# Five more projections of the first layer take the paired form on the tensor engine

## The chip, the core and the metric

The kernel runs on one core of a Trainium2 chip. The engines named here are TensorE (PE in the profile; its weight loads are PEld), VectorE (DVE), ScalarE (ACT), GpSimd (POOL) and SyncE (SP, which here only issues DMAs). Each works through a list of instructions of its own and waits on the others through semaphores. The metric is the device time of one execution in microseconds.

## The reference

A trunk of two layers works on x of 256 x 1024 in float32. In each layer one normalised x goes through one combined input projection, and its 3584 columns feed three branches: dilated attention (8 heads), a gated linear recurrence (width 256) and stick-breaking attention (4 heads). Each branch is multiplied by a SiLU gate, and all of them go through the output projection back onto x.

```
hn = rms_norm(x, norm_gain)
proj = jnp.einsum('bsd,de->bse', hn, w_in)
a_q, a_k, a_v, a_g, b_x, b_g, c_q, c_k, c_v, c_g = jnp.split(proj, _in_split_points(), axis=-1)
y_a = dilated_attention(rope(a_q), rope(a_k), a_v) * jax.nn.silu(a_g)
y_b = rg_lru_branch(b_x, conv_w, conv_b, ...) * jax.nn.silu(b_g)
y_c = stick_breaking_attention(c_q, c_k, c_v) * jax.nn.silu(c_g)
x = x + jnp.einsum('bse,ed->bsd', concat([y_a, y_b, y_c]), w_out)
```

## The kernel before

**Products.** To keep float32 accuracy, every operand is split into a rounded part and its rest (x into `xh` and `xl`, a weight into `whi` and `wlo`), and three products are summed: rounded by rounded, rounded by rest, rest by rounded. `xh` and `xl` of the same 128 rows lie side by side in the tile `xx`, each 256 positions wide.

**Chunks.** The columns of the input projection come in chunks of 256, in a fixed order: stick-breaking q and k (CQ, CK), first dilated q and k (heads 0 to 3; AQ0, AK0), the recurrent input (BX), second dilated q and k (AQ1, AK1), the stick-breaking gate (CG), the recurrent gate (BG), two chunks of the dilated gate (AG, AG+1), then four chunks of the output projection. A chunk's weights arrive in two DMAs of 512 KB into the tiles `st` (5 of them); ScalarE rounds each quarter into `whi` (L115), VectorE subtracts to get `wlo` (L117). `whi` and `wlo` have 4 buffers each; `st` is free for the next load once L117 has read it, so loads wait on VectorE. Each chunk's weights are asked for two chunks ahead (`AHEAD`).

**Two forms of a chunk** (`proj_b`). A chunk has two halves of 128 columns. The narrow form makes 24 products of 256 columns for each half (L225) and keeps both halves in one PSUM bank of the pool `pp`. The paired form makes, for each half, 8 products 512 columns wide of `whi` with `xx`, which gives the first and the rest of x at once (L344), and 8 of 256 columns of `wlo` with `xh` (L341). The half has a bank of its own; its two sides are summed afterwards: ScalarE copies one side into the tile `low` (L347), VectorE adds it to the other (L349). Layer 1 uses the paired form for all its chunks, layer 0 so far only for the two dilated gate chunks (`PAIRED`). `pp` has three banks. A bank can be taken again only when the sum L349 (paired) or the operations that read it (narrow) are done.

**Normalisation in layer 0.** x goes into the products unnormalised; the reciprocal norms, as a row `rb`, are multiplied in afterwards (`scaled` at L413, `rotated` at L514 and L518). Layer 1 has no such product.

**Order of the work.** TensorE's instructions stand in the order in which the code writes them; VectorE's and ScalarE's lists are put together by a scheduler when the kernel is built, and are then fixed. Between the two halves of some chunks other work is put in (`mid`): in AQ1 `second()`, the scores of the first dilated heads (L542 on TensorE, then L549 and the softmax on VectorE and ScalarE), and in BG `third()`, the recurrent gates (L601), the values of two branches (L453, one of them in a bank of `pp`) and the scores of the second dilated heads (L542). The dilated probabilities are turned by L489.

Of the kernel before, what the change touches and what calls it, by code (L numbers as in the profile page):

```python
# [15 lines left out]
P = 128  # L16
S = 256
# [25 lines left out]

CH_AV, CH_CV, CH_CQ, CH_CK, CH_BX, CH_CG, CH_BG, CH_AG, CH_O = 0, 2, 3, 4, 7, 10, 11, 12, 14
CH_AQ, CH_AK = (5, 8), (6, 9)
PAIRED = ((CH_AG, CH_AG + 1), (CH_CQ, CH_CK, CH_AQ[0], CH_AK[0], CH_BX, CH_AQ[1], CH_AK[1], CH_CG, CH_BG, CH_AG, CH_AG + 1))


@with_exitstack
def trunk_kernel(ctx: ExitStack, tc: tile.TileContext, x, first_x, first, wpack, prm_d, gatew, gains, consts, rope, out):  # L50
    nc = tc.nc
    act, dve, pe, gps = nc.scalar, nc.vector, nc.tensor, nc.gpsimd
# [13 lines left out]
    def scr(w):  # L66
        return wk.tile([P, 512], F32, name="scr", tag="scr", bufs=SCR)[:, 0:w]
# [20 lines left out]
    def v2(a, n=2):  # L88
        return a.rearrange("p (b t) -> p b t", b=n)
# [58 lines left out]
    pair = None  # L148
    for k in range(NK):
# [5 lines left out]
        if k % 2 == 0:  # L155
            pair = [wsp.tile([P, 2048], F32R, name=n, tag=n) for n in ("whi", "wlo")]
        o = k % 2
# [150 lines left out]
    rb = cst.tile([P, S], F32, name="rb")  # L308
    gn = cst.tile([P, D], F32, name="gn", tag="gn")

    for l in range(L):
# [14 lines left out]
        def proj_b(c, mid=None, to=None, sc=1.0):  # L326
            pair = c in PAIRED[l]
            hi, lo = [a.rearrange("p (k c) -> p k c", c=256) for a in weights(l, c, AHEAD - 1 if mid else AHEAD)]
# [29 lines left out]
            return flat  # L358

        def proj_to(dst, c, mid=None, sc=1.0):  # L360
            if l > 0 and c in PAIRED[l]:
                proj_b(c, mid, [dst[:, b, :] for b in range(2)], sc)
            else:
                scaled(dst, proj_b(c, mid), sc)

# [44 lines left out]
        def scaled(dst, ps, sc=1.0):  # L410
            if l == 0:
                a, b = rows(ps)
                dve.scalar_tensor_tensor(dst, a, sc, b, ALU.mult, ALU.mult)  # L413
            else:
                act.activation(dst, v2(ps), AF.Copy, scale=sc)
# [9 lines left out]
        if l > 0:  # L425
            tables()

        def silu(dst, ps):
            sg = v2(scr(512))
            src = v2(ps)  # L430
            if l == 0:
                src = v2(scr(512))
                scaled(src, ps)
            tab(sg, src, AF.Sigmoid)
            dve.tensor_mul(dst, src, sg)

# [66 lines left out]
        def rotated(c, tiles, h0, tag, mid=None):  # L503
            dst = tiles[h0] = sb.tile([P, 2, S], F32, name=tag, tag=tag)
            tab_ = rp0 if l == 0 else rp
            if l > 0:
                src = scr(S)
                proj_b(c, mid, [src, dst[:, 1, :]])
            else:
                ps = proj_b(c, mid)  # L510
                src = ps[:, 0:S]
            sh = scr(S)
            dve.stream_shuffle(sh, src, SHUF)
            dve.tensor_mul(dst[:, 0, :], src, tab_[:, 0, :])  # L514
            dve.tensor_mul(sh, sh, tab_[:, 1, :])
            dve.tensor_add(dst[:, 0, :], dst[:, 0, :], sh)
            if l == 0:
                dve.tensor_mul(dst[:, 1, :], ps[:, S:2 * S], rb)  # L518

        qT, kT, exact = {}, {}, {}  # L520
        prob = {}
# [59 lines left out]
        bg = sb.tile([P, 2, S], F32, name="bg", tag="bg")  # L581
        cg = sb.tile([P, 2, S], F32, name="cg", tag="cg")
# [74 lines left out]
        rotated(CH_AK[1], kT, 4, "k1")  # L657
        split_qk(4, ("q0", "ag"))
        table(SIGM)
        cg_ps = proj_b(CH_CG)  # L660
        pts = dil_transposes(0)
        silu(cg, cg_ps)


# [5 lines left out]
            y_c["y"] = values(va, pts, 0, bank(pp, "pp"))  # L670
            y_c["s"] = dil_scores(4)

        silu(bg, proj_b(CH_BG, third))
        y_half(1)
        table(LN_EXP)
        lru_scan()
# [2 lines left out]
        ps = None  # L679
        if CH_AG in PAIRED[l]:  # L680
            agf = sb.tile([P, 2, S], F32, name="agf", tag="cg")
            proj_b(CH_AG, None, [agf[:, b, :] for b in range(2)])
            ps = agf.rearrange("p b t -> p (b t)")
        dil_softmax(y_c["s"])
        ps = proj_b(CH_AG) if ps is None else ps
# [168 lines left out]
```

## Time and profile before

| | |
|---|---|
| median of 3 runs (lowest to highest) | 246.11 us (246.09 to 246.35) |
| the profiled execution's own time | 246.06 us |
| its span in the profile | 244.2 us |
| busy share of the span: PE, PEld, DVE, ACT, POOL | 97%, 85%, 82%, 71%, 4% |
| layer 0 from its first chunk to the end of AG+1, by the chain of waits | 23.63 to 98.24 us |
| granted TensorE clock | 0.999 |

Times in the views are microseconds from the span's start. In a row of a timeline stand start, duration, engine, line, operation, output and inputs, the count, and in brackets how long the engine was idle before and what ended that. Several rows of equal instructions are merged; the start of the next row shows how long they took together, since an instruction's last part overlaps the next one's first. In the chain of waits stand start, duration, and what ran.

### The profile page before, as it was taken

What the parts mean: (1) busy time and instruction counts of PE and PEld (TensorE: products, weight loads), DVE (VectorE), ACT (ScalarE), POOL (GpSimd) and SP (SyncE); (2) the same over time, 40 slices, a digit from 0 to 9 for tenths busy, and PEclk for the clock granted to TensorE, in tenths of its full rate; (3) what the DMA queues carried; (4) which work ended last, traced back from release to release, by engine and by line L of the source; (5) the groups of instructions that cost most, each with busy time, mean ns of one, the idle gap of its engine ahead of it and who ended that gap; (6) DMA issues with size and microseconds to landing.
All of it is one profiled execution on the core that took longest, in us unless ns stands there. A gap on an engine that the chain in (4) does not pass through costs nothing.

```text
span 244.2 us, 4576 instructions
## 1 busy us (share of the span) xinstructions
PE 236.2 (97%) x1651; PEld 206.6 (85%) x1651; DVE 200.0 (82%) x480; ACT 174.4 (71%) x384; POOL 10.5 (4%) x43
## 2 busy tenths in 40 slices
PE   8799999999999999999999999999999999999991
PEld 4588999999999798878888888888888878887881
DVE  3694699999999889999495585999999986997362
ACT  3677987919597689994673674876669867998143
POOL 0017200002000000000000000000010000000000
PEclk9999999999999999999999999999999999999999
DMA  6989988565846843068448288615470771000022
GB/s 193 377 254 390 384 268 291 190 205 177 240 152 207 272 153 105 1 195 320 175 134 273 88 289 268 199 44 177 171 214 7 226 282 63 31 0 0 3 75 97
DMA packets 14037, 43.89 MB, mean 180 GB/s; under 512 B 1728, under 2 KB 3008, under 8 KB 14016
## 3 DMA queue, kind: packets, MB, share of 16 engines
q1 hardware_dynamic: 13248, 42.43, 51.9%
q0 software_dynamic: 192, 0.52, 0.8%
q10 hardware_dynamic: 576, 0.66, 0.7%
q8 instruction: 13, 0.21, 0.4%
q14 instruction: 8, 0.07, 0.1%
HBM read 42.03 MB, written 1.05 MB: 176 GB/s over the span
## 4 chain that ended last, share of the span: by engine, by line
PE 94%; DMA 3%; DVE 1%; SPq 0%; ACT 0%; issue 0%; DVEq 0%
PE pp L225 34%; PE pp L344 20%; PE pp L341 10%; PE s L225 9%; PE s L181 4%; PE s L489 3%; DMA st<-first 3%; PE y L453 2%; PE pp L383 2%; PE s L542 2%; PE pp L181 2%; PE s L469 1%; PE y L225 1%; PE pp L453 1%; PE s L601 1%; PE s L273 1%
## 5 line engine op out<-in xcount | busy, mean ns | idle before, releaser
L117 DVE TENSOR_TENSOR wlo<-st,whi 128x512 fp32r<-128x512 f32 x128 | 81.8, 684 | 7.5 <-ACT whi L115 6.9
L115 ACT ACTIVATE whi<-st 128x512 fp32r<-128x512 f32 x130 | 72.5, 627 | 9.0 <-DMA st<-w_pack 3.4
L344 PE MATMUL pp<-xx,whi 128*128 128x512 f32 x208 | 50.8, 393 | 0.0
L344 PEld LDWEIGHTS pp<-xx,whi 128*128 128x128 f32 x208 | 37.8, 188 | 7.6 <-DVE q L349 0.3
L225 PE MATMUL pp<-xx,whi 128*128 128x256 f32 x288 | 38.2, 285 | 0.0
L225 PEld LDWEIGHTS pp<-xx,whi 128*128 128x128 f32 x288 | 35.8, 191 | 0.8 <-issue 0.3
L341 PEld LDWEIGHTS pp<-xx,wlo 128*128 128x128 f32 x208 | 26.9, 191 | 1.6 <-ACT scr L84 0.3
L341 PE MATMUL pp<-xx,wlo 128*128 128x256 f32 x208 | 28.0, 284 | 0.0
L225 PE MATMUL pp<-xx,wlo 128*128 128x256 f32 x144 | 20.2, 283 | 0.0
L84 ACT ACTIVATE pr<-scr,mn 128x128 f32<-128x128 f32 (+1 forms) x32 | 14.1, 443 | 6.6 <-DVE mn L549 6.6
L225 PEld LDWEIGHTS pp<-xx,wlo 128*128 128x128 f32 x144 | 18.6, 192 | 0.0
L78 ACT ACT_TABLE_LOAD x13 | 16.7, 1283 | 1.9 <-PEq L847 1.7
L347 ACT ACTIVATE low<-pp 128x256 f32<-128x256 f32 x26 | 9.4, 373 | 8.8 <-PE pp L344 8.0
L225 PE MATMUL pp<-whi,yh 128*128 128x512 f32 (+1 forms) x48 | 14.1, 382 | 0.0
L225 PE MATMUL pp<-wlo,yh 128*128 128x512 f32 (+1 forms) x48 | 13.7, 372 | 0.0
L225 PE MATMUL pp<-whi,yl 128*128 128x512 f32 (+1 forms) x48 | 13.6, 371 | 0.0
L181 PE MATMUL s<-whi,xx 128*128 128x512 f32 (+1 forms) x36 | 9.6, 384 | 1.8 <-ACT xx L161 1.7
L225 PEld LDWEIGHTS pp<-whi,yl 128*128 128x128 f32 x48 | 8.6, 188 | 1.6
L225 PEld LDWEIGHTS pp<-wlo,yh 128*128 128x128 f32 x48 | 8.6, 188 | 1.6
L225 PEld LDWEIGHTS pp<-whi,yh 128*128 128x128 f32 x48 | 8.3, 188 | 1.6 <-issue 0.3
L549 DVE CUSTOM_DVE_ANT_0 scr<-s,con 128x128 f32<-128x128 f32 (+1 forms) x32 | 9.2, 350 | 0.0
L181 PEld LDWEIGHTS s<-whi,xx 128*128 128x128 f32 x36 | 6.0, 197 | 3.3 <-ACT xx L161 2.5
(189 smaller groups left out, 372.3 us busy)
## 6 DMA issues: line engine op xcount, KB each, us to landing
st<-w_pack SPq DMA_DIRECT2D x66, 512.0 KB, 5.3
st<-first SPq DMA_DIRECT2D x7, 512.0 KB, 7.0
xres<-x_in SPq DMA_DIRECT2D x4, 256.0 KB, 7.5
gw_t<-gate_w SPq DMA_DIRECT2D x2, 256.0 KB, 6.8
gn<-gains SPq DMA_DIRECT2D x2, 256.0 KB, 5.9
xs<-xc POOLq DMA_DIRECT2D x4, 128.0 KB, 3.8
gf<-gains SPq DMA_DIRECT2D x2, 256.0 KB, 5.4
out<-st ACTq DMA_DIRECT2D x2, 192.0 KB, 2.0
```

The source lines that it names most:

```text
L78: load = act.preload_act_table_set(name)
L84: i = dep(act.activation(*a, **k), loaded["load"])
L115: split[l, c] = act.activation(h, part, AF.Copy)
L117: dve.tensor_sub(r, part, h.bitcast(F32))
L181: pe.matmul(ps[t][:, c0:c1], a[:, k, t * P:(t + 1) * P], b, start=k == 0 and all(m[0] is not ps for m in seq[:i]), stop=k == NK - 1 and al ...
L225: pe.matmul(ps, a(k), b(k), start=first and i == 0, stop=last and i == len(seq) - 1, skip_group_check=skip)
L341: pe.matmul(ps[:, 0:S], lo[:, k, cs], xh[:, k, :], start=i == 0, stop=i == len(seq) - 1, skip_group_check=True)
L344: pe.matmul(ps, hi[:, k, cs], xx[:, k].rearrange("p h t -> p (h t)"), start=i == 0, stop=i == len(seq) - 1, skip_group_check=True)
L347: act.activation(low, ps[:, S:2 * S], AF.Copy, scale=sc)
L453: pe.matmul(y[hr, p * 128 + o:p * 128 + 256], vt[:, s0, hs], wts[i][s0], start=s0 == 0, stop=s0 == 1)
L489: pe.transpose(tp[:, i * P:(i + 1) * P], tiles[h0 + h][:, j * P:(j + 1) * P], ident)
L549: dve.tensor_tensor_reduce(xs[:, cs], sps[h][:, cs], nmask[:, cs], -0.125, 3e38, ALU.add, ALU.min, mn[:, t:t + 1])
```

## The change

In layer 0, BX, AQ1, AK1, CG and BG go from the narrow to the paired form. The sums of their halves are written where the value is to live (the convolution's input, the rotated tiles, the gates' own tiles); the product with `rb` is then made from there and no longer from PSUM. For BX that is a product in place (`proj_to`), for the gates `scaled` reads the gate's tile, for q and k the first half is summed into scratch before the rotation and the second half into its home.

```diff
-PAIRED = ((CH_AG, CH_AG + 1), (CH_CQ, CH_CK, CH_AQ[0], CH_AK[0], CH_BX, CH_AQ[1], CH_AK[1], CH_CG, CH_BG, CH_AG, CH_AG + 1))
+PAIRED = ((CH_BX, CH_AQ[1], CH_AK[1], CH_CG, CH_BG, CH_AG, CH_AG + 1), (CH_CQ, CH_CK, CH_AQ[0], CH_AK[0], CH_BX, CH_AQ[1], CH_AK[1], CH_CG, CH_BG, CH_AG, CH_AG + 1))
...
         def proj_to(dst, c, mid=None, sc=1.0):
-            if l > 0 and c in PAIRED[l]:
+            if c in PAIRED[l]:
                 proj_b(c, mid, [dst[:, b, :] for b in range(2)], sc)
+                if l == 0:
+                    dve.tensor_mul(dst, dst, rb.rearrange("p (o t) -> p o t", o=1).broadcast_to([P, 2, S]))
...
+        def home(tile_):
+            return [tile_[:, b, :] for b in range(2)] if l == 0 else None
+
         def silu(dst, ps):
             sg = v2(scr(512))
-            src = v2(ps)
+            src = dst if ps is None else v2(ps)
             if l == 0:
-                src = v2(scr(512))
-                scaled(src, ps)
+                ps, src = src, v2(scr(512))
+                scaled(src, ps.rearrange("p b t -> p (b t)"))
...
-            if l > 0:
-                src = scr(S)
-                proj_b(c, mid, [src, dst[:, 1, :]])
+            pair = c in PAIRED[l]
+            if pair:
+                src, high = scr(S), dst[:, 1, :]
+                proj_b(c, mid, [src, high])
             else:
                 ps = proj_b(c, mid)
-                src = ps[:, 0:S]
+                src, high = ps[:, 0:S], ps[:, S:2 * S]
...
             if l == 0:
-                dve.tensor_mul(dst[:, 1, :], ps[:, S:2 * S], rb)
+                dve.tensor_mul(dst[:, 1, :], high, rb)
...
-        cg_ps = proj_b(CH_CG)
+        cg_ps = proj_b(CH_CG, None, home(cg))
...
-        silu(bg, proj_b(CH_BG, third))
+        silu(bg, proj_b(CH_BG, third, home(bg)))
```

Ten sums (L349) and ten copies (L347) are added to the lists of VectorE and ScalarE, and the scheduler puts these lists together anew. Three places on VectorE follow, each before and then in the changed kernel. Lines behind the first edits have other numbers in the changed kernel: L513 to L518 are L519 to L524, L549 is L555, L413 is L415, L435 is L440, L562 is L568, L590 is L596, L617 is L623. An `ISA` row is the reduction of scores (L549).

First place: from the split of the first dilated k, over BX and its convolution, to the first reduction of scores. Before:

```order
L528 TENSOR_TENSOR qk_717<-k_644,qk_717 128x512
L117 TENSOR_TENSOR wlo<-st,whi 128x512 x2
L413 SCALAR_TENSOR_TENSOR bxp<-pp,rb 128x2x256
L588 TENSOR_SCALAR xc<-bxp,prm_t 128x256 x2
L590 SCALAR_TENSOR_TENSOR xc<-bxp,prm_t,xc 128x256 x2
L117 TENSOR_TENSOR wlo<-st,whi 128x512
L590 SCALAR_TENSOR_TENSOR xc<-bxp,prm_t,xc 128x256 x4
L117 TENSOR_TENSOR wlo<-st,whi 128x512 x7
L549 ISA scr,mn<-s,con 128x128
```

The same place in the changed kernel:

```order
L534 TENSOR_TENSOR qk_717<-k_644,qk_717 128x512
L349 TENSOR_TENSOR bxp<-pp,low 128x256
L117 TENSOR_TENSOR wlo<-st,whi 128x512 x2
L349 TENSOR_TENSOR bxp<-pp,low 128x256
L364 TENSOR_TENSOR bxp<-bxp,rb 128x2x256
L594 TENSOR_SCALAR xc<-bxp,prm_t 128x256 x2
L117 TENSOR_TENSOR wlo<-st,whi 128x512
L596 SCALAR_TENSOR_TENSOR xc<-bxp,prm_t,xc 128x256 x6
L349 TENSOR_TENSOR scr<-pp,low 128x256
L117 TENSOR_TENSOR wlo<-st,whi 128x512 x4
L520 TENSOR_TENSOR q_805<-scr,rp_288 128x256
L555 ISA scr,mn<-s,con 128x128
```

Three sums and a product of the rotation now stand ahead of the first reduction, and four weight splits in place of seven.

Second place: from the end of the first softmax to the rotation of the second dilated k (`q_814` and `q_805` are the second dilated q, `k_948` the second dilated k). Before:

```order
L562 TENSOR_SCALAR pr<-pr,den 128x256
L514 TENSOR_TENSOR q_814<-pp,rp_288 128x256
L515 TENSOR_TENSOR scr<-scr,rp_288 128x256
L518 TENSOR_TENSOR q_814<-pp,rb 128x256
L516 TENSOR_TENSOR q_814<-q_814,scr 128x256
L117 TENSOR_TENSOR wlo<-st,whi 128x512
L528 TENSOR_TENSOR qk_1035<-q_814,qk_1035 128x256
L117 TENSOR_TENSOR wlo<-st,whi 128x512
L513 STREAM_SHUFFLE scr<-pp 128x256
```

The same place in the changed kernel:

```order
L568 TENSOR_SCALAR pr<-pr,den 128x256
L349 TENSOR_TENSOR q_805<-pp,low 128x256
L522 TENSOR_TENSOR q_805<-q_805,scr 128x256
L524 TENSOR_TENSOR q_805<-q_805,rb 128x256
L117 TENSOR_TENSOR wlo<-st,whi 128x512 x4
L349 TENSOR_TENSOR scr<-pp,low 128x256
L349 TENSOR_TENSOR k_948<-pp,low 128x256
L519 STREAM_SHUFFLE scr<-scr 128x256
```

The sum of AQ1's second half stands behind the whole softmax, and four weight splits stand between it and the sums of AK1's two halves. By the banks that the built kernels use, the first half of CG takes the bank of AQ1's second half, the second half of CG that of AK1's first half, and BG's first half that of AK1's second.

Third place: from the last reduction of the second scores to the sum of AG's first half (`agf`). Before:

```order
L549 ISA mn 128x1
L413 SCALAR_TENSOR_TENSOR scr<-pp,rb 128x512
L117 TENSOR_TENSOR wlo<-st,whi 128x512 x2
L435 TENSOR_TENSOR bg<-scr 128x512
L117 TENSOR_TENSOR wlo<-st,whi 128x512 x2
L617 TENSOR_TENSOR scr<-av 128x512
L349 TENSOR_TENSOR agf<-pp,low 128x256
```

The same place in the changed kernel:

```order
L555 ISA mn 128x1
L349 TENSOR_TENSOR bg<-pp,low 128x256
L415 SCALAR_TENSOR_TENSOR scr<-bg,rb 128x512
L117 TENSOR_TENSOR wlo<-st,whi 128x512 x2
L440 TENSOR_TENSOR bg<-scr 128x512
L117 TENSOR_TENSOR wlo<-st,whi 128x512
L623 TENSOR_TENSOR scr<-av 128x512
L349 TENSOR_TENSOR agf<-pp,low 128x256
```

The sum of BG's second half stands ahead of the gate's product with `rb`, and one weight split has gone behind. The first half of AG+1 takes the bank of AG's first half in the changed kernel as before it.

## The prediction

> **What bounds the kernel now.** I read the page first: its span, the busy shares, VectorE's slices and the chain that ended last.
>
> ```profile
> span 244.2 us, 4576 instructions
> PE 236.2 (97%) x1651; PEld 206.6 (85%) x1651; DVE 200.0 (82%) x480; ACT 174.4 (71%) x384; POOL 10.5 (4%) x43
> DVE  3694699999999889999495585999999986997362
> PE 94%; DMA 3%; DVE 1%; SPq 0%; ACT 0%; issue 0%; DVEq 0%
> ```
>
> TensorE sets the time: 94% of the chain is its own work. But from the sixth slice to the thirteenth (6.1 us each, 30 to 79 us) VectorE stands at 9 as well, so it is the second bound of just the stretch that is changed. The windows of that stretch say how full it is; the columns behind the times are length, then PE, PEld, DVE and ACT busy.
>
> ```profile
> 51.68:58.75 7.07, 7.07 (x65) 6.94 (x62) 7.03 (x17) 4.39 (x9) 0.41 (x4) 1.00 0.56 186
> 58.75:64.40 5.65, 5.65 (x76) 5.51 (x77) 5.65 (x16) 2.95 (x8) 1.25 (x2) 1.00 0.81 243
> 64.40:70.20 5.80, 5.80 (x50) 5.80 (x50) 5.80 (x31) 5.77 (x19) 0.00 (x0) 1.00 0.76 254
> ```
>
> VectorE has 0.04 us free in 18.5; ScalarE has 5.4. Next the chain in order of time, for layer 0 and, below the second dots, two pieces of layer 1, which has the paired form already.
>
> ```profile
> 32.71 5.75 PE pp L225 x48
> ...
> 58.75 1.37 PE s L542 x38
> 60.12 14.59 PE pp L225 x120
> 74.71 1.31 PE s L489 x12
> 76.02 2.86 PE pp L225 x24
> 78.88 1.02 PE s L601 x16
> ...
> 84.02 3.06 PE pp L225 x24
> 87.08 1.84 PE pp L344 x8
> 88.92 1.91 PE pp L341 x16
> 90.83 3.65 PE pp L344 x16
> ...
> 98.24 2.73 PE s L225 x12
> ...
> 183.01 3.83 PE pp L344 x16
> ...
> 206.57 3.70 PE pp L344 x16
> ```
>
> TensorE runs through layer 0 without a gap. In layer 1, 16 wide products take 3.83 us once and 3.70 once, against 3.65 in AG: 0.18 and 0.05 us lost, both where a half must wait for a bank.
>
> **What the change saves.** A narrow half is 24 products: 5.75 / 2 = 2.88 us. A paired half is 8 wide, 3.65 / 2 = 1.83, and 8 narrow, 1.91 / 2 = 0.95: 2.78 us. Columns streamed are as many as before (12288 per chunk); only the cost per product falls away, for 8 products fewer: 0.10 us per half, 1.0 us for ten. The Trainium skill (TensorE: Matmul & The Clock Gate, section "Wait — 56ns, not 53.3ns?") has the start-to-start time of a warm product at its columns over 2.4 GHz plus 2.5 ns; by that rule the saving would be an estimated 10 x 8 x 2.5 ns = 0.2 us, and rivals 1 and 2 below would come out 0.8 us later. The rows give 120 ns for 256 columns and 228 for 512, so 11 to 12 ns per product here; I go by them.
>
> **What it adds.** Per form, from the grouped view:
>
> ```profile
> L117 DVE TENSOR_TENSOR wlo<-st,whi 128x512 fp32r<-128x512 f32 x128 | 81.8, 684 | 7.5 <-ACT whi L115 6.9
> L347 ACT ACTIVATE low<-pp 128x256 f32<-128x256 f32 x26 | 9.4, 373 | 8.8 <-PE pp L344 8.0 <-PE pp L341 0.8
> L349 DVE TENSOR_TENSOR scr<-pp,low 128x256 f32<-128x256 f32 x12 | 4.9, 418 | 0.7 <-ACT low L347 0.7
> ```
>
> Ten copies are 3.7 us on ScalarE, which lie in its free time. Ten sums are 10 x 0.42 on a VectorE that has no free time. The products with `rb` and the rotation cost the same from either memory, so they are moved, not added, save that BX's product now must wait for its sum. Banks matter more: a paired half gives its bank back only after copy and sum, and the sums stand in VectorE's list behind other work. So I walk VectorE's list of the changed kernel with the durations of before. These rows are VectorE's, layer 0 and, below the first dots, layer 1, with one row of PEld last.
>
> ```profile
> 53.23 0.68 DVE L528 TENSOR_TENSOR qk<-k,qk 128x512 fp32r<-128x512 f32 x1
> 55.77 0.74 DVE L588 TENSOR_SCALAR xc<-bxp,prm_t 128x256 f32<-128x256 f32 x2
> 59.40 4.29 DVE L117 TENSOR_TENSOR wlo<-st,whi 128x512 fp32r<-128x512 f32 x7
> 63.62 0.28 DVE L549 CUSTOM_DVE_ANT_0 scr<-s,con 128x128 f32<-128x128 f32 x1
> ...
> 178.61 0.42 DVE L514 TENSOR_TENSOR q<-scr,rp 128x256 f32<-128x256 f32 x1
> 178.94 0.28 DVE L549 CUSTOM_DVE_ANT_0 scr<-s,con 128x128 f32<-128x128 f32 x1
> ...
> 184.25 0.42 DVE L349 TENSOR_TENSOR q<-pp,low 128x256 f32<-128x256 f32 x1
> ...
> 184.72 1.69 PEld L344 LDWEIGHTS pp<-xx,whi 128*128 128x128 f32 x8 [0.30 <-DVE q L349]
> ```
>
> Start to start, a split costs 0.60 us ((63.62 - 59.40) / 7) and a 256-wide operation 0.33. Before, the scores of the first dilated heads were done at 60.12, but their reduction began at 63.62, behind seven splits: the order of the list decides, not readiness.
>
> *First bank (CG's first half waits for the sum of AQ1's second half).* The split of k starts at 53.23 as before, the next at 53.84. Sum 0.33, two splits 1.2, sum 0.5 with its wait for `low` and for its result, product 0.73: L588 starts at 56.6, 0.85 later than before. Its convolution and one split take 3.63 (55.77 to 59.40): 60.25. Sum 0.33, four splits 2.4, rotation 0.33: the reduction starts at 63.35. From there the list is layer 1's, where the sum starts 5.31 us later (178.94 to 184.25) and ends at 0.42: bank free at 69.1. TensorE: three halves have gained 0.3 by then, so the scores run 58.45 to 59.82; AQ1's second half takes 2.98 (layer 0 has the same 0.2 after L542: 3.06 against 2.88), AK1 5.56: it wants the bank at 68.36. In layer 1 the products start 0.35 after the sum's end (184.67 to 183.01 + 1.83 + 0.18 = 185.02), so here at 69.45. **Stall 1.1 us.**
>
> *Second bank (CG's second half waits for the sum of AK1's first half).* After 68.7 come the sum, two operations and four splits: 3 x 0.33 + 2.4, then this sum 0.42: free at 72.5, products at 72.9. TensorE wants it at 69.45 + 2.78 = 72.25. **Stall 0.65 us.**
>
> *Third bank (AG+1's first half waits for the sum of AG's first half).* Rows of before, VectorE first, then ScalarE:
>
> ```profile
> 84.44 0.28 DVE L549 CUSTOM_DVE_ANT_0 scr<-s,con 128x128 f32<-128x128 f32 x1
> ...
> 87.12 0.69 DVE L413 SCALAR_TENSOR_TENSOR scr<-pp,rb 128x512 f32<-128x512 f32 x1 [0.38 <-PE pp L225]
> ...
> 91.74 0.42 DVE L349 TENSOR_TENSOR agf<-pp,low 128x256 f32<-128x256 f32 x1
> ...
> 117.64 0.69 DVE L744 TENSOR_TENSOR xres<-pp,xres 128x512 f32<-128x512 f32 x1 [1.67 <-PE pp L225]
> ...
> 88.26 0.61 ACT L84 ACTIVATE scr<-scr 128x512 f32<-128x512 f32 x1
> 88.89 1.28 ACT L78 ACT_TABLE_LOAD   x1
> ```
>
> Before, that sum ended at 92.16, and 0.35 later is 92.51; TensorE came at 87.08 + 5.57 = 92.65. The margin is 0.15 us. Now: from 72.45 VectorE has ten 256-wide operations (3.3) and eighteen 512-wide ones, twelve of them splits (10.8), and some 0.3 of waits until the second reductions: 86.9, where before it was 84.44. The reductions take 2.3 (87.12 - 0.38 - 84.44); the sum of BG's second half 0.45: the gate's product starts at 89.65. From there to AG's sum it was 4.62 (87.12 to 91.74); the sigmoid had waited 0.45 for ScalarE's splits (87.81 to 88.26) and now doesn't: 4.17. Sum at 93.8 to 94.25, products at 94.6. TensorE: CG ends at 72.9 + 2.78 = 75.7, L489 1.31, BG's first half 2.78, `third()` 5.14 (78.88 to 84.02), the second half 2.98, AG 5.56: 93.45. **Stall 1.15 us.**
>
> Behind it AG+1 takes 5.56 and ends at 100.15, against 98.24: later by 1.9 us. The sum of terms is the same: -1.0 + 1.1 + 0.65 + 1.15 = +1.9. What follows is off by as much on both engines, and VectorE waits for TensorE again by 117.64 (1.67 us), so the lag doesn't grow into layer 1, whose code is untouched. From the profiled execution, 246.06 us (0.05 below the median), that is **248.0 us**.
>
> **Bounds.** Saving: 0.2 below the rows' 1.0 at the worst, if the changes between wide and narrow cost more than in AG. Stalls: at least layer 1's, 0.18, 0 and 0.05; at most 0.6 more each than walked, since some 110 instructions stand in the walk. Where a stall ends on VectorE's row, TensorE's saving ahead of it doesn't count: the end of AG+1 hangs on the last stall alone, and an error of 1% in VectorE's 40 us is 0.4 us. The forecast's own range is 247.2 to 248.8.
>
> A load is the other unknown: those for AG+1 now stand behind splits that come later, and its second half can be issued at about 71.1 (the second of BG's splits), where ScalarE needs it by 74.9 ahead of the rounding of k. A load that had the queue for itself before:
>
> ```profile
> L108 SPq DMA_DIRECT2D st<-w_pack x1: 328/328/328, 72.5 to 72.5; - x1
> DMA to landing us min/median/max: 3.8/3.8/3.8
> ```
>
> At 3.8 us it lands at 74.9, just in time.
>
> **The rivals.**
> (1) *Sums hidden as in layer 1*: banks are late by 0.18 and 0.05 only, -1.0 + 0.23 = -0.8: 245.3. For it: layer 1 does the same chunks at that loss. Against: VectorE there has no products with `rb`, and the sums don't stand behind four splits.
> (2) *VectorE keeps pace, but the gate's chain is longer*: BG's copy and sum come ahead of the gate's product, 0.37 + 0.42. Products after AG's sum came 5.43 after BG's end (92.51 - 87.08), now 6.22, or 5.77 without the sigmoid's wait; TensorE comes 5.57 after it, so AG+1 stalls 0.2 to 0.65. With 0.2 at CG that is -1.0 + 0.4 to 0.85, or 245.5 to 245.9. For it: that margin. Against: the walk, by which the reductions are 2.5 us late.
> (3) *Weights late*: the load for AG+1 takes 4.7 us or more instead of 3.8; ScalarE's list stands still until it lands, the rounding of k, the second scores and AG's sum come 0.9 later at least, on top of the forecast: 248.9 upwards. For it: two loads are now issued 1.2 us apart. Against: at 72 us the queue is nearly empty.
>
> **How the numbers follow.** Forecast 0.76, rival 1 0.04, rival 2 0.10, rival 3 0.10. About 0.2% (0.5 us) is what a measurement of this kernel can tell from no change. Faster holds rival 1 and a part of rival 2: 0.08; the same holds most of rival 2 and the forecast's low edge: 0.07; slower the rest, 0.85. The range runs from 246.5, above rivals 1 and 2, to 249.2, into rival 3.
>
> **What would show it.** Right: in the chain, halves of L344 and L341 at 2.78 us; PEld waiting for L349 of q ahead of CG (1.1 us), of scr ahead of CG's second half (0.65) and of agf ahead of AG+1 (1.15); VectorE without a gap from 45 to 87 us; the second reductions near 87. Wrong: PEld waits there under 0.3 us, or the reductions start by 85 (rivals 1 and 2); ScalarE waiting for `st<-w_pack` near 75 us (rival 3); or TensorE stalled for another cause, a missing `wlo` say.

## The result, and the profile after

The changed kernel takes 247.47 us in the median (nine runs, 246.78 to 248.64), the kernel before 246.11: a ratio of 1.0067, 95% interval 1.0042 to 1.0092. It is slower by 0.4 to 0.9%; 248.0 was forecast. The profiled execution took 246.81 us. Its page, the rows that answer to those of before:

```profile
span 244.9 us, 4428 instructions
PE 236.6 (97%) x1571; PEld 202.9 (83%) x1571; DVE 203.1 (83%) x490; ACT 177.3 (72%) x394; POOL 10.5 (4%) x43
DVE  3884798999999999999695485899999986997362
PE 83%; DVE 10%; ACT 2%; DMA 2%; issue 0%; SPq 0%; DVEq 0%
```

TensorE's share of the chain fell from 94% to 83%, and VectorE's rose from 1% to 10%: the end now hangs on VectorE for a while. The chain in order of time says where (start, duration, what ran):

```profile
31.43 0.23 PE y L401 x2
...
47.76 1.84 PE pp L344 x8
49.60 0.95 PE pp L341 x8
...
64.60 1.57 ACT pr L84 x7
...
68.59 2.41 DVE wlo L117 x4
...
93.08 2.11 PE pp L344 x8
...
98.94 2.73 PE s L225 x12
...
108.47 1.45 PE y L458 x16
```

A paired half is 1.84 + 0.95 = 2.79 us, as worked out. But from 64.60 to 93.08 the chain has no TensorE in it. TensorE itself waits three times in that time, at the three places that were named. Its weight loads, with the wait ahead of them in brackets:

```profile
67.97 1.68 PEld L344 LDWEIGHTS pp<-xx,whi 128*128 128x128 f32 x8 [1.04 <-DVE q L349]
...
71.39 1.02 PEld L341 LDWEIGHTS pp<-xx,wlo 128*128 128x128 f32 x8 [0.56 <-DVE scr L349]
...
93.08 1.68 PEld L344 LDWEIGHTS pp<-xx,whi 128*128 128x128 f32 x8 [1.24 <-DVE agf L349]
```

**How much the stretch lost.** The two profiled executions do not start alike, mostly because the first loads landed 0.84 us sooner in this one (5.41 us for 6.25 in the chain). So each execution is measured from the first product of the rows of norms, the row `31.43 ... PE y L401 x2`, to the values of the first branch behind AG+1, the row `108.47 ... PE y L458 x16`: 77.04 us. In the kernel before, the same rows stand at 32.48 and 107.77, with other line numbers: 75.29. The stretch is 1.75 us longer. What follows is as long as before to a tenth (244.9 - 108.47 = 136.43, and 244.2 - 107.77 = 136.43), and the earlier start hides 1.05. The same stretch by engine, columns as in the prediction's windows, first of before, then of after:

```profile
32.48:107.77 75.29, 75.29 (x645) 69.89 (x645) 72.14 (x184) 59.74 (x129) 1.66 (x6) 1.00 0.57 185
```
```profile
31.43:108.47 77.04, 75.26 (x564) 65.53 (x565) 74.38 (x193) 61.24 (x137) 1.67 (x6) 1.00 0.55 178
```

VectorE has 2.24 us more to do in it and takes 1.75 us longer; its free time falls from 3.15 us to 2.66. Whether this added work sets the loss or the three waits do is what the experiments ask.

### The profile page after: what moved, and what is told of

Its sections match the earlier page's. It is cut to its first block, busy times and chain, and to the rows that moved or that the text cites. A ratio compares the mean times of both kernels' runs of the same rounds, so it can differ in the third digit from the quotient of the medians.

```text
span 244.9 us, 4428 instructions
## 1 busy us (share of the span) xinstructions
PE 236.6 (97%) x1571; PEld 202.9 (83%) x1571; DVE 203.1 (83%) x490; ACT 177.3 (72%) x394; POOL 10.5 (4%) x43
## 3 DMA queue, kind: packets, MB, share of 16 engines
HBM read 42.03 MB, written 1.05 MB: 176 GB/s over the span
## 4 chain that ended last, share of the span: by engine, by line
PE 83%; DVE 10%; ACT 2%; DMA 2%; issue 0%; SPq 0%; DVEq 0%
PE pp L225 22%; PE pp L344 22%; PE pp L341 12%; PE s L225 9%; PE s L181 4%; DVE wlo L117 4%; PE s L494 3%; PE pp L385 2%; DMA st<-first 2%; PE pp L181 2%; PE y L458 2%; PE s L548 2%; PE s L474 1%; PE y L225 1%; DVE scr L555 1%; PE s L273 1%
## 5 line engine op out<-in xcount | busy, mean ns | idle before, releaser
L117 DVE TENSOR_TENSOR wlo<-st,whi 128x512 fp32r<-128x512 f32 x128 | 82.0, 683 | 8.1 <-ACT whi L115 7.5
L115 ACT ACTIVATE whi<-st 128x512 fp32r<-128x512 f32 x130 | 73.2, 628 | 8.7 <-DMA st<-w_pack 5.0
L344 PE MATMUL pp<-xx,whi 128*128 128x512 f32 x288 | 71.0, 394 | 1.4 <-DVE agf L349 0.8
L344 PEld LDWEIGHTS pp<-xx,whi 128*128 128x128 f32 x288 | 52.2, 188 | 12.4 <-DVE agf L349 1.4
L341 PEld LDWEIGHTS pp<-xx,wlo 128*128 128x128 f32 x288 | 37.3, 191 | 2.9 <-DVE scr L349 0.6
L347 ACT ACTIVATE low<-pp 128x256 f32<-128x256 f32 x36 | 13.2, 373 | 11.5 <-PE pp L344 10.7
L225 PE MATMUL pp<-xx,whi 128*128 128x256 f32 x128 | 16.8, 284 | 0.0
L225 PEld LDWEIGHTS pp<-xx,whi 128*128 128x128 f32 x128 | 15.9, 192 | 0.3 <-issue 0.3
L181 PE MATMUL s<-whi,xx 128*128 128x512 f32 (+1 forms) x36 | 10.4, 411 | 0.3 <-ACT xx L161 0.2
L555 DVE CUSTOM_DVE_ANT_0 scr<-s,con 128x128 f32<-128x128 f32 (+1 forms) x32 | 9.2, 351 | 0.0
L485 DVE TENSOR_TENSOR_SCAN sw<-scr,con 128x127 f32<-128x127 f32 (+1 forms) x16 | 8.0, 539 | 0.7 <-ACT scr L84 0.7
L568 DVE TENSOR_SCALAR pr<-pr,den 128x128 f32<-128x128 f32 (+1 forms) x32 | 8.4, 314 | 0.2
```

The source lines that it names most:

```text
L115: split[l, c] = act.activation(h, part, AF.Copy)
L117: dve.tensor_sub(r, part, h.bitcast(F32))
L181: pe.matmul(ps[t][:, c0:c1], a[:, k, t * P:(t + 1) * P], b, start=k == 0 and all(m[0] is not ps for m in seq[:i]), stop=k == NK - 1 and al ...
L225: pe.matmul(ps, a(k), b(k), start=first and i == 0, stop=last and i == len(seq) - 1, skip_group_check=skip)
L341: pe.matmul(ps[:, 0:S], lo[:, k, cs], xh[:, k, :], start=i == 0, stop=i == len(seq) - 1, skip_group_check=True)
L344: pe.matmul(ps, hi[:, k, cs], xx[:, k].rearrange("p h t -> p (h t)"), start=i == 0, stop=i == len(seq) - 1, skip_group_check=True)
```

## The experiments

Two readings were open. In one, each of the three waits is a loss of its own, and an order that takes one away gets its time back. In the other, VectorE's list sets the end, and a wait only shows where TensorE meets it. A third question was whether the kernel could keep the saving at all. In the table stand the ratio to the kernel before in runs on the same chip, then what the stretch of the last section lost against 75.29 us, and how much of it VectorE was free, both by the profiled execution. From the stretch's end to layer 1's first product are 33.50 us in the kernel before, in the change and in all other runs of the table that have a trace, but for three: e10, e11 and e12 lose 0.32, 0.10 and 0.38 us more there.

| run | ratio [95%] | stretch | VectorE free |
|---|---|---|---|
| the change | 1.0067 [1.0042, 1.0092] | +1.75 | 2.66 |
| e1_early_q_k_sums | 1.0057 [1.0035, 1.0078] | +1.52 | 3.05 |
| e2_early_ag_sum | 1.0081 [1.0056, 1.0106] | +1.86 | 2.26 |
| e3_all_three | 1.0073 [1.0052, 1.0094] | +1.85 | 2.53 |
| e4_no_sums | 1.0011 [0.9997, 1.0024] | +0.25 | 4.49 |
| e5_ten_more_sums | 1.0088 [1.0076, 1.0100] | +1.79 | 2.39 |
| e6_six_rests_on_gpsimd | 1.0144 [1.0125, 1.0163] | +4.73 | 5.37 |
| e7_bx_aq1_ak1_paired | 1.0038 [1.0023, 1.0054] | +0.92 | 3.00 |
| e8_cg_bg_paired | 1.0086 [1.0069, 1.0102] | +1.60 | 4.71 |
| e9_no_sums_o0_later | 1.0001 [0.9986, 1.0017] | – | – |
| e10_o0_later | 1.0126 [1.0105, 1.0146] | +2.44 | 5.89 |
| e11_q_k_sums_and_o0 | 1.0071 [1.0049, 1.0093] | +1.31 | 3.82 |
| e12_rewritten_lists | 1.0036 [1.0017, 1.0054] | +0.61 | 2.42 |

e9 has no trace of an ordinary execution, so its last two fields are empty. In the diffs, `dep(a, b)` puts `a` behind `b` in the order that the scheduler makes, and nothing else; `lows`, `sums`, `rests` and `rounds` hold a chunk's copies (L347), sums (L349), splits (L117) and roundings (L115), `soft` the named instructions of softmax and gates. O0 and O1 are the first two chunks of the output projection.

### Taking the waits away by order: e1, e2, e3

e1 puts AQ1's second copy ahead of the softmax's exponentials, its second sum ahead of the reciprocals, and BG's four splits behind AK1's first sum:

```diff
-        rotated(CH_AQ[1], qT, 4, "q1", second)
+        rotated(CH_AQ[1], qT, 4, "q1", second); l == 0 and [dep(soft[0, k][0], d[0, CH_AQ[1], 1]) for k, d in (("exp", lows), ("rec", sums))]
...
-        split_qk(4, ("q0", "ag"))
+        split_qk(4, ("q0", "ag")); l == 0 and [dep(i, sums[0, CH_AK[1], 0]) for i in rests[0, CH_BG]]
```

> Order alone: ScalarE's copy of AQ1's second half is put ahead of the softmax's exponentials, its sum ahead of the reciprocals, and the four splits of BG's weights behind the sum of AK1's first half. Theory (VectorE has no free time, so the end of AG+1 hangs on its row alone): the two waits ahead of CG fall from 1.04 and 0.56 us to under 0.3 each, but AG's sum stands where it stood on VectorE, within 0.3 us, so the wait ahead of AG+1 grows from 1.24 to some 2.5 us and the time stays at 247.2 to 247.5. Rival (each wait is a loss of its own): the third wait stays at 1.2 and the time falls by 1.6, to 245.9.

Both waits ahead of CG's halves are gone, 1.60 us of them, and the stretch is 0.23 us shorter than in the change. These are TensorE's waits now:

```profile
81.41 0.29 PEld L548 LDWEIGHTS s<-k,q 32*128 32x128 f32 x2 [0.50 <-ACT rt L84]
82.14 0.41 PEld L548 LDWEIGHTS s<-k,q 32*128 32x128 f32 x9 [0.44 <-ACT it L84]
...
92.67 1.68 PEld L344 LDWEIGHTS pp<-xx,whi 128*128 128x128 f32 x8 [0.99 <-DVE agf L349]
```

TensorE came to the second scores (those of the second dilated heads) sooner and waited there for the recurrent gates (`rt`, `it`), which ScalarE makes behind its other work. The wait ahead of AG+1, expected to grow to 2.5 us, fell to 0.99; the time stayed where it was expected. The page of this kernel gives VectorE 21% of the chain, in the change 10%. e2 takes the third wait away: ScalarE copies AG's first half ahead of a change of its function table.

```diff
-            proj_b(CH_AG, None, [agf[:, b, :] for b in range(2)])
+            proj_b(CH_AG, None, [agf[:, b, :] for b in range(2)]); l == 0 and dep(loaded["load"], lows[0, CH_AG, 0])
```

> Order alone: ScalarE's copy of AG's first half is put ahead of the load of the exponential's table, so that its sum comes before the product of av. Theory: the wait ahead of AG+1 falls from 1.24 us to under 0.3; the next that is late is the rest of the recurrent gate's part of y (now done 0.35 us before TensorE uses it), so the gain is 0.4 to 0.9: 246.6 to 247.1. Rival (each wait a loss of its own): 1.15 gained, 246.3. Rival (VectorE's fill alone counts, whatever the order): 247.4.

AG+1 no longer waits, and the stretch is no shorter; the expected gain of 0.4 to 0.9 us did not come. The next products wait instead, for the recurrent branch's rounded output and for the gate's product that frees their bank:

```profile
99.61 0.30 PEld L225 LDWEIGHTS s<-whi,yh 128*128 128x128 f32 x2 [0.96 <-ACT yh L446]
100.67 0.30 PEld L225 LDWEIGHTS s<-whi,yl 128*128 128x128 f32 x2 [0.31 <-DVE yl L447]
...
102.75 0.30 PEld L225 LDWEIGHTS pp<-whi,yh 128*128 128x128 f32 x2 [0.26 <-DVE scr L444]
```

0.96 + 0.31 + 0.26 = 1.53, for 1.24 taken away. The chain ahead of that rounded output runs on ScalarE from 88.89 to 96.09, over a rounding, a change of table, exponentials and the recurrent branch's `th`, so here the order on ScalarE counts and not VectorE's fill alone. e3 has both edits:

```diff
+        rotated(CH_AQ[1], qT, 4, "q1", second); l == 0 and [dep(soft[0, k][0], d[0, CH_AQ[1], 1]) for k, d in (("exp", lows), ("rec", sums))]
...
+        split_qk(4, ("q0", "ag")); l == 0 and [dep(i, sums[0, CH_AK[1], 0]) for i in rests[0, CH_BG]]
...
+            proj_b(CH_AG, None, [agf[:, b, :] for b in range(2)]); l == 0 and dep(loaded["load"], lows[0, CH_AG, 0])
```

> Both edits of order together. Theory (VectorE too full): the waits ahead of CG under 0.3 us, the one ahead of AG+1 0.5 to 1.5, since TensorE now comes 1.6 us earlier than VectorE's list can serve it, or the wait moves on to the parts of y in the output's products; 246.3 to 246.9. Rival (each wait a loss of its own): all 2.8 us gained, 244.7, below the kernel before.

All three bank waits are gone, and the time is that of the change. Its weight loads wait 0.37 and 0.44 us at the second scores, then 0.79, 0.30 and 0.27 at the places of e2. The first reading falls: the waits are not three losses that can be had back.

### The sums without the pairing, the pairing without the sums: e5, e4

e5 is the kernel before with ten 256-wide additions on VectorE, at the places of the sums and with nothing paired:

```diff
+        def more(tile_):
+            for b in range(2 if l == 0 else 0):
+                dve.tensor_add(wk.tile([P, S], F32, name="low", tag="low", bufs=2), tile_[:, b, 0:S], tile_[:, b, 0:S])
...
+            more(bxp)
...
```

> The kernel before, all chunks narrow as they were, with ten additions of 128x256 more on VectorE (two behind each of BX, AQ1, AK1, CG and BG, from and to on-chip memory, their result unused). No bank is handed back another way, and TensorE saves nothing. Theory (VectorE's fill from 38 to 92 us is the whole cause, and TensorE's saving doesn't count because VectorE sets the end): VectorE reaches AG's sum 1.5 to 2.2 us later and the ratio is that of the changed kernel, 1.005 to 1.009. Rival (what costs is that banks come back only after copy and sum): 1.000 to 1.002.

It loses as much as the change, 1.0088 against 1.0067, with intervals that overlap. TensorE has no wait at CG and one at AG+1:

```profile
93.48 1.69 PEld L344 LDWEIGHTS pp<-xx,whi 128*128 128x128 f32 x8 [1.43 <-DVE agf L349]
```

So ten short operations on VectorE cost this kernel some 2 us (248.03 against 245.97) with the banks of the five chunks handed back as before; the wait turns up at the bank of AG, which was paired already. e4 does the reverse: the five chunks stay paired, but ScalarE copies the first side home, and the second side, rest of x by rounded weight, is left out with its sums.

```diff
-                    act.activation(low, ps[:, S:2 * S], AF.Copy, scale=sc)
-                    if sc == 1.0:
+                    act.activation(*((to[b], ps[:, 0:S]) if l == 0 and c < CH_AG else (low, ps[:, S:2 * S])), AF.Copy, scale=sc)
+                    if sc == 1.0 and (l > 0 or c >= CH_AG):
...
```

> In BX, AQ1, AK1, CG and BG the sum is left out: ScalarE copies the first 256 columns of the bank straight to their home, and the product of the rest of x with the weights' high part is left out of the result (TensorE still makes it). Theory (the ten sums on VectorE are the cause): VectorE has 3.3 us less to do, the three waits fall under 0.3 us each, TensorE keeps its saving of 1.0 us: 245.1 (244.8 to 245.6). Rival (TensorE saves nothing, or the paired products cost more than their rows say): no wait, but 246.1 or more. Rival (the copies on ScalarE hold the banks): the wait ahead of CG stays at 0.5 us or more.

Without the sums the loss is gone, and there is no gain either (245.1 us had been expected, 245.82 came where the kernel before took 245.5). TensorE was ahead: its products for the recurrent gates (the first with `gw_t`) start at 77.27, 45.56 us into the stretch, where before it was 46.33 (78.81 - 32.48). It then waits at the second scores, and by 0.17 us at AG+1; besides a wait of 0.35 us at the stretch's end, which the kernel before has too, only these weight loads show a wait for another engine:

```profile
82.13 0.41 PEld L548 LDWEIGHTS s<-k,q 32*128 32x128 f32 x9 [0.44 <-ACT it L84]
...
91.86 1.69 PEld L344 LDWEIGHTS pp<-xx,whi 128*128 128x128 f32 x8 [0.17 <-DVE agf L349]
```

By the products' starts, the second scores take 2.44 us to the next product (81.04 to 83.48), where before it was 1.36 (82.59 to 83.95): 1.08 us lost in that one place. VectorE, then ScalarE, ahead of it:

```profile
73.83 3.69 DVE L117 TENSOR_TENSOR wlo<-st,whi 128x512 fp32r<-128x512 f32 x6
77.44 0.69 DVE L415 SCALAR_TENSOR_TENSOR scr<-cg,rb 128x512 f32<-128x512 f32 x1
...
78.16 0.63 ACT L84 ACTIVATE scr<-scr 128x512 f32<-128x512 f32 x1 [1.64 <-DVE scr L415]
78.70 1.66 ACT L115 ACTIVATE whi<-st 128x512 fp32r<-128x512 f32 x3
...
80.53 0.83 ACT L84 ACTIVATE rt<-s,prm_t 128x256 f32<-128x256 f32 x2
```

CG's product with `rb` stands behind six splits in VectorE's list (behind three in the change). CG's sigmoid on ScalarE waits 1.64 us for it, and behind the sigmoid stand three roundings of O0 and a copy, and only then the gates. VectorE is free for 4.49 us of the stretch, so what is late here is late by its place in a list. It also shows a limit of e4 and e5: the scheduler laid the lists of both anew, and they differ in more than the sums.

### Less work on VectorE: e6, e7, e8

e6 gives six of twelve splits of BG, AG and AG+1 to GpSimd, that is 6 x 0.60 = 3.6 us off VectorE.

```diff
-                dve.tensor_sub(r, part, h.bitcast(F32))
+                (gps if l == 0 and c in (CH_BG, CH_AG, CH_AG + 1) and j else dve).tensor_sub(r, part, h.bitcast(F32))
```

> The changed kernel, but six of the twelve splits of the weights of BG, AG and AG+1 (the second half of each load) are made on GpSimd, whose queue has little else; VectorE loses 6 x 0.60 = 3.6 us of work, as much as the ten sums brought. Theory: VectorE is as early at AG's sum as before the change, the wait ahead of AG+1 falls under 0.5 us, and the ratio falls to 0.998 to 1.003. Rival (the two engines slow each other, or GpSimd takes so long that TensorE or ScalarE waits for a rest): 1.006 or more, with a wait for wlo on TensorE. Not seen in the trace so far: how long GpSimd takes for 128x512.

It is the slowest of all. The rival's time came, though TensorE waits for no `wlo`. GpSimd's timeline, and VectorE's at the same time:

```profile
69.74 4.61 POOL L117 TENSOR_TENSOR wlo<-st,whi 128x512 fp32r<-128x512 f32 x3 [4.53 <-ACT whi L115]
```
```profile
70.56 1.19 DVE L534 TENSOR_TENSOR qk<-q,qk 128x256 fp32r<-128x256 f32 x1
72.02 1.17 DVE L520 TENSOR_TENSOR k<-scr,rp 128x256 f32<-128x256 f32 x1
73.11 0.41 DVE L349 TENSOR_TENSOR k<-pp,low 128x256 f32<-128x256 f32 x1
73.45 1.19 DVE L521 TENSOR_TENSOR scr<-scr,rp 128x256 f32<-128x256 f32 x1
...
77.03 1.78 DVE L534 TENSOR_TENSOR qk<-k,qk 128x512 fp32r<-128x512 f32 x1
```

TensorE's weight loads of the second scores:

```profile
84.08 0.29 PEld L548 LDWEIGHTS s<-k,q 32*128 32x128 f32 x2 [1.60 <-ACT rt L84]
84.81 0.41 PEld L548 LDWEIGHTS s<-k,q 32*128 32x128 f32 x9 [0.44 <-ACT it L84]
```

In the change the four VectorE operations at L534, L520, L521 and again L534 take 0.41, 0.40, 0.41 and 0.69 us. Here they take 3.4 us more together, which is nearly all of the 3.6 taken off, while GpSimd needs about 1.5 us in this row for a split that VectorE does in 0.68. The gates come later for it, TensorE waits 2.04 us in 2.5, and then something more follows, which the windows show:

```profile
82.00:84.00 2.00, 0.67 (x10) 0.31 (x6) 2.00 (x5) 2.00 (x6) 0.00 (x0) 1.00 0.95 373
84.00:86.00 2.00, 1.68 (x35) 1.49 (x36) 1.55 (x3) 1.55 (x5) 0.00 (x0) 0.95 0.91 268
86.00:88.00 2.00, 2.00 (x13) 1.78 (x9) 1.30 (x7) 0.63 (x1) 0.00 (x0) 0.50 0.82 288
88.00:90.00 2.00, 2.00 (x9) 1.67 (x8) 1.69 (x14) 0.00 (x0) 0.00 (x0) 0.70 0.28 106
```

The granted clock, the third column from the right, falls to half.

e7 and e8 pair only some of the five chunks (`home` gives none for the others; the line that is replaced is that of the change):

```diff
+PAIRED = ((CH_BX, CH_AQ[1], CH_AK[1], CH_AG, CH_AG + 1), (CH_CQ, CH_CK, CH_AQ[0], CH_AK[0], CH_BX, CH_AQ[1], CH_AK[1], CH_CG, CH_BG, CH_AG, CH_AG + 1))
```
```diff
+PAIRED = ((CH_CG, CH_BG, CH_AG, CH_AG + 1), (CH_CQ, CH_CK, CH_AQ[0], CH_AK[0], CH_BX, CH_AQ[1], CH_AK[1], CH_CG, CH_BG, CH_AG, CH_AG + 1))
```

> Only BX, AQ1 and AK1 are paired; CG and BG are as before. Six sums in place of ten, 2.0 us in place of 3.3; in the changed kernel 1.4 of the 3.3 was taken up by waits that VectorE had, and 1.9 arrived at AG's sum. Theory (a dose): 2.0 - 1.4 = 0.6 late at AG's sum, less the margin of 0.15: ratio 1.001 to 1.003. Rival (each bank wait a loss of its own): the wait of CG stays at 1.0 us, the saving of six halves is 0.6 and there is none at AG+1, so +0.4 too, but with the wait ahead of CG and not ahead of AG+1.

> Only CG and BG are paired; BX, AQ1 and AK1 are as before. Four sums, 1.3 us, less than the 1.4 that VectorE's waits took up. Theory (a dose): nothing late at AG's sum but what BG's copy and sum put into the gate's chain (0.2 to 0.65 by the prediction's second rival), less TensorE's saving of 0.4 where it counts: ratio 0.999 to 1.002. Rival (the gates' pairing is what costs): 1.004 or more.

A loss by the number of sums alone is refuted: the ratio is 1.0086 with four sums (e8) and 1.0038 with six (e7). Nor do the parts add: the stretch loses 0.92 + 1.60 = 2.52 us in the two, 1.75 in the change. In e7 both of its readings are half right: the wait ahead of CG stays at 1.03 us, as the rival had it, and one of 0.70 stands ahead of AG+1, as the theory had it. The chain passes a weight load, which is rival 3's mechanism:

```profile
72.46 4.37 DMA st<-w_pack
```

In e8 VectorE is free for 4.71 us of the stretch, and the chain ahead of AG+1 goes over ScalarE. BG ends, its second half is copied, three roundings and the sigmoid come, the table changes, and AG's sum stands behind what that releases:

```profile
86.22 1.85 PE pp L344 x8
...
88.09 0.38 ACT low L347
88.48 1.56 ACT whi L115 x3
...
90.58 1.28 ACT L78
...
93.51 0.35 DVE agf L349
...
93.90 2.11 PE pp L344 x8
```

From BG's end (88.07) to AG+1's products are 5.83 us. Rival 2 had put that at 5.77 to 6.22. It is only a part of e8's loss: the weight loads wait 0.33 and 0.44 us at the second scores and 0.70 at AG+1. The theory's 0.999 to 1.002 was missed, and its rival's 1.004 or more came; which of CG and BG costs the more is not shown.

### Can the saving be kept: e9 to e12

The roundings and splits of O0, which nothing needs soon, stand in these lists ahead of the gates and of AG's sums. e9 is e4 with the roundings behind the gates, e10 the change with that and with O0's splits behind AG's first sum, and e11 is e10 with the edits of e1 and O1's splits behind that sum too (the first line below is in all three, the second in e10 and e11, the third in e11):

```diff
-            ps = agf.rearrange("p b t -> p (b t)")
+            ps = agf.rearrange("p b t -> p (b t)"); l == 0 and [dep(r, soft[0, "gate"]) for r in rounds[0, CH_O]]
...
-        table(SIGM)
+        table(SIGM); l == 0 and [dep(r, sums[0, CH_AG, 0]) for r in rests[0, CH_O]]
...
-        silu(ag[:, 2:4, :], seeded)
+        silu(ag[:, 2:4, :], seeded); l == 0 and [dep(r, sums[0, CH_AG, 0]) for r in rests[0, CH_O + 1]]
```

> The kernel without the ten sums again (the product of the rest of x with the weights' high part left out of BX, AQ1, AK1, CG and BG), with the four roundings of O0's weights, which TensorE uses only after AG+1, put behind the recurrent gates on ScalarE. Without that, the gates stood behind three of these roundings, the second scores waited for the gates' banks, and what TensorE had saved by then (0.85 us) was lost there. Theory (the saving is real and was lost in that wait): ratio 0.996 to 0.999. Rival (the saving can't be had here at all, another wait takes it): 1.000 to 1.002.

> The changed kernel with all its sums; the only edits are of order: O0's roundings behind the recurrent gates on ScalarE, and O0's four splits, 2.4 us, behind the sum of AG's first half on VectorE. Theory (the list, not the amount of work, makes the third wait): the second reductions start some 2.5 us earlier, the wait ahead of AG+1 falls from 1.24 to under 0.4; the two waits ahead of CG stay: ratio 1.002 to 1.004. Rival (VectorE is too full in any order): the parts of y or O0's rests come late by as much, 1.006 or more.

> Both together: the order of the first experiment (sums of AQ1 and AK1 early) and O0's and O1's roundings and splits put back. Theory: the waits ahead of CG under 0.3 us, that ahead of AG+1 under 0.8, and TensorE keeps a part of its 1.0 us: ratio 0.997 to 1.001, at or below the kernel before. Rival (VectorE is too full in any order): 1.005 or more, with the wait at the parts of y or at O0's rests.

e9 takes the same time as the kernel before; where its saving goes stays open, since no trace shows it. e10 is worse. Its second reductions start 1.5 us earlier in the stretch (84.58 - 31.83 for 85.71 - 31.43) and the wait ahead of AG+1 falls to 0.69 us, but the four splits that went behind AG's first sum now stand ahead of its second, and the second half of AG+1 waits for that. Chain:

```profile
93.46 2.41 DVE wlo L117 x4
...
96.47 0.35 DVE agf L349
...
96.96 1.20 PE pp L341 x8
```

e11 has no wait at CG, 0.75 us at AG+1 and again 1.15 at its second half. e12 has e3's edits, and its lists were put right place by place: O0's roundings and BG's first copy behind the gates, O0's splits (but one) behind BG's product with `rb`, O1's splits behind the recurrent branch's output, the rounding of that output ahead of the sigmoid's table, O1's last two roundings and one exponential behind `th`.

```diff
+        silu(bg, proj_b(CH_BG, third, home(bg))); scaled_bg = soft.get((0, "scaled"))
...
+        emit_y(rt, bg, 2, 2); rest_y, round_y = soft[l, "yl"], soft[l, "yh"]
...
+        table(SIGM, [round_y] if l == 0 else ()); l == 0 and [dep(r, b) for r, b in [(i, soft[0, "gate"]) for i in rounds[0, CH_O] + [lows[0, CH_BG, 0]]] + [(i, scaled_bg) for i in rests[0, CH_O][1:]] + [(soft[0, "exp"][11], soft[0, "th"])]]
...
+        silu(ag[:, 2:4, :], seeded); l == 0 and [dep(r, b) for r, b in [(i, rest_y) for i in rests[0, CH_O + 1]] + [(i, soft[0, "th"]) for i in rounds[0, CH_O + 1][2:]]]
```

> The changed kernel with all sums and its work unchanged; the lists of ScalarE and VectorE between AQ1 and O1 are rewritten by hand after the waits that the earlier runs showed: sums of AQ1 and AK1 early; BG's first copy behind the recurrent gates; AG's first copy ahead of the exponential's table; O0's roundings behind the gates and its splits in VectorE's pauses around BG's gate, not between AG's two sums; O1's splits behind the recurrent gate's part of y; that part's rounding ahead of the sigmoid's table. Theory (order can only win back what VectorE's pauses of some 3 us between 83 and 92 us hold): the waits ahead of CG and AG+1 all under 0.4 us, ratio 0.996 to 1.000. Rival (VectorE and ScalarE are too full from 38 to 105 us in any order, and a wait that is taken away turns up behind): 1.003 or more, with the wait now at the parts of y, at O1's rests or at the output's banks.

It is the best with all five chunks paired: 246.74 us, ratio 1.0036, about half the loss. By the starts of the products in the timeline, the first one behind AG+1 stands 64.94 us into the stretch (97.04 - 32.10), where before it was 65.76 (98.08 - 32.32): up to there TensorE waits for no other engine, and 0.82 us of the saving is kept. Then:

```profile
102.43 0.30 PEld L225 LDWEIGHTS pp<-whi,yh 128*128 128x128 f32 x2 [1.39 <-DVE scr L444]
```

The bank of the next products is held until VectorE has multiplied by the dilated gate, and 1.39 us goes back in one wait. Behind the stretch it loses 0.38 us more (142.04 - 108.16 = 33.88 us to layer 1's first product, for 33.50). So its rival came, the wait at the output's bank included. No version here beats the kernel before.

**What is settled.** With the sums left out the loss is gone (e4), and ten such operations without the pairing cost as much (e5): the sums on VectorE are what costs, as far as two kernels whose lists were laid anew can show it. The runs refute that the three waits (e1 to e3), or the number of sums (e7, e8), are prices that add.

Whether VectorE's list sets the end differs from run to run. In the change and in e5 the chain ahead of AG+1 is VectorE's list with few breaks: in e5 from 61.89 to 93.44 with 0.64 us of ScalarE in it, in the change from 66.19 to 93.03 with 0.64 and 2.83. In e2, e3 and e12 VectorE is as full (free for 2.3 to 2.5 us of the stretch, as in the change and e5, 2.4 to 2.7), but their chains then turn to ScalarE's list for 7.2, 7.2 and 6.4 us ahead of what is late. So a full VectorE alone doesn't say which engine the end hangs on. In e4, e8, e10 and e11 VectorE is free for 3.8 to 5.9 us, and what is late is one operation behind another in ScalarE's list or in VectorE's own: order, not amount. So neither of the two readings holds alone. e12's stretch is 1.14 us shorter than the change's; 0.90 of that is VectorE's work that went behind it (73.48 us busy against 74.38), and a third of the gain is lost again there. The expected times came in e1 and e5 only; all the others had expected less loss than came, e7 by a hair.

## Why the prediction was right, and where it was loose

**The size.** +1.9 was forecast for the stretch, +1.75 came; 247.47 lies in the forecast's own range. The medians differ by 1.36 us, and the ratio's interval (1.0 to 2.3 us) holds all three.

**The walk along VectorE's list** carried it. In the change's timeline VectorE's steps start as follows; the walk's times, on the clock of before, are to be taken 1.05 earlier:

```profile
62.20 0.29 DVE L555 CUSTOM_DVE_ANT_0 scr<-s,con 128x128 f32<-128x128 f32 x1
...
67.51 0.41 DVE L349 TENSOR_TENSOR q<-pp,low 128x256 f32<-128x256 f32 x1
...
85.71 0.28 DVE L555 CUSTOM_DVE_ANT_0 scr<-s,con 128x128 f32<-128x128 f32 x1
...
92.61 0.42 DVE L349 TENSOR_TENSOR agf<-pp,low 128x256 f32<-128x256 f32 x1
```

First reductions at 63.35 - 1.05 = 62.30 (came 62.20), second at 85.85 (85.71), AG's sum at 92.75 (92.61): never more than 0.14 us off over 30 us. The list's order with the durations of before was enough. VectorE without a gap was a sign as well: of the 42 us named, on the change's clock 43.95 to 85.95, it is busy for 41.60.

**The three waits**: 1.1, 0.65 and 1.15 forecast, 1.04, 0.56 and 1.24 measured, each released by the sum that was named. These are waits of the weight loads, which run ahead of the products; with the saving that e12 shows, the products lost 1.75 + 0.82 = 2.57 us, where the terms have 2.9. So both sides of the sum were about 0.2 to 0.35 too large, and that they cancelled was luck. As an account of TensorE's time it adds up. As causes they do not add: the text's sum -1.0 + 1.1 + 0.65 + 1.15 reads as if each had its price, and e1 to e3 show that it does not. The sentence in the bounds, that the end of AG+1 hangs on the last stall alone, was nearer, and still too narrow: with that stall gone too (e2, e3) the next one took its place.

**The saving** of 1.0 us is TensorE's. 0.82 of it was to be seen where nothing made TensorE wait (e12, at the end of AG+1), which lies within the 0.2 that the bounds allowed; none of it reached the end of a kernel.

**What follows.** "The lag doesn't grow into layer 1" held: 136.43 us before and after, with spans known to a tenth, and 33.50 of them to layer 1's first product in both.

**The rivals.** Rival 1's 245.3 was not reached even with the sums left out (e4, 245.82 in runs where before took 245.5). Rival 2's longer gate chain lay right under the walk: it is what AG+1 meets in e8, e10 and e11. Rival 3's sign was badly chosen. ScalarE did wait for a load near 74 us in the change:

```profile
73.70 0.63 ACT L115 ACTIVATE whi<-st 128x512 fp32r<-128x512 f32 x1 [1.89 <-DMA st<-w_pack]
```

But VectorE's operation that needs the rounding of k behind it started at 74.89, 1.29 us after two splits that take 1.20: it cost 0.09. In e7 a load in the same place was on the chain.

## What to carry to other kernels

Where a second engine is full over the stretch of a change, price the change by what it adds to that engine's list, and walk that list in its built order with measured durations. Waits of the first engine that all trace back to a full second one are not separate losses: take one away, and look for the next place where the two meet before counting the gain. Work that nothing needs soon can be ordered behind what frees a bank, on both engines that empty the banks: here that won back about half the loss once (e12) and made it worse when the work landed ahead of the next sum (e10). Expect each such edit to bring out the next place.

## What the runs showed that was not expected

**VectorE beside GpSimd (e6).** VectorE operations with both inputs in the on-chip memory went from 0.40 to 0.69 us to 1.17 to 1.78 while GpSimd worked, and one that reads `pp` and one other tile stayed at 0.41. The Trainium skill (SBUF — State Buffer, section "Who interferes with whom") says that a VectorE instruction with two inputs in the on-chip memory SBUF contends with a GpSimd instruction that reads SBUF, and that one with at most one such input, outside the modes that use two ports, does not; these rows agree.

**The clock after a wait (e6).** TensorE waited 1.60 and 0.44 us within 2.5, and the granted clock then was 0.95, 0.50 and 0.70 in three windows of 2 us, which is half speed for 0.2 + 2.0 + 1.2 = 3.4 us if the clock stood either at full or at half. Sixteen products took 2.00 + 2.27 us (chain, from 86.45), for 0.95 + 1.84 in the change: 1.5 us more. In the change, with waits of 1.04, 0.56 and 1.24 us, the clock stayed at 1.00 over the whole stretch. The Trainium skill (TensorE: Matmul & The Clock Gate, section "What's actually happening") has the clock at half after an idle window of about 3.4 us. The time at half speed agrees with that length; the waits ahead of it were shorter than the window, so by that rule a window need not be idle throughout; how busy it may be no run here shows.
